# Up-projection of a hybrid layer: adding a stored product on VectorE, and weight differences on GpSimd

## Chip, core and metric

The kernel runs on one core of a Trainium2 chip. The metric is the device time of one execution in microseconds, lower is better. Engines are called TensorE (PE), VectorE (DVE), ScalarE (ACT), GpSimd (POOL) and SyncE (SP, which issues most of the DMAs). The profile's L-numbers are line numbers of the kernel before.

## What is computed

One transformer layer on a sequence of 1024 positions and a width of 1024, all in float32. It normalises the input, mixes tokens (an mLSTM head group beside sliding-window attention), adds the result to the input, and then runs a gated MLP with a short convolution. The change touches the up-projection of that MLP:

```python
def conv_ffn(h, w_up, conv_w, conv_b, w_down):
    u = causal_dwconv(h @ w_up, conv_w, conv_b)
    g, val = u[..., :D_FF], u[..., D_FF:]
    return (jax.nn.gelu(g, approximate=True) * val) @ w_down
```

D_FF is 2816, so w_up has 5632 columns: 2816 for the gate g and 2816 for val. The convolution has width 3 along positions.

## The kernel before

**Chunks.** The up-projection runs over 22 chunks (`up`, L1083). Chunk j makes 128 gate columns and the matching 128 val columns for all 1024 positions. A tile has the 128 columns as partitions and the positions along its free axis, in halves of 512.

**Seven products instead of eight.** For a chunk the 2x2 block product (two halves of the positions, gate and val, two halves of the inner dimension) is written in Strassen's way, in Winograd's form. Seven products of halves are made, each from a left side (sums and differences of the normalised input, S1 to S4, A11, A12, A22, made once) and a right side (weights, or differences of weights). Sums of products then give the four output quarters. Products are named by number 1 to 7; the dict `left` (L1038) names the left side of each. Products 4, 5, 6 and 7 use weight differences.

**Three matmuls for each k.** A float32 operand is split into a high part (a cast on ScalarE) and a remainder (a subtraction on VectorE, both in `split`, L86). One product is then 4 inner blocks by 3 matmuls (L1049 to L1051): high by high, high by remainder, remainder by high.

**Weight differences.** `up_tees` (L925) makes the four differences T of a chunk from its raw gate and val tiles (`fu` in the profile, loaded on L922): t0 = b12 - b11, t1 = b22 - t0, t2 = b22 - b12, t3 = b21 - t1, each 128x512, in L931 to L934. t1 depends on t0 and t3 on t1. There is one buffer for them (tags mix3 and mix4), so a chunk's differences wait until those of the chunk before are split. `fensure` (L938) prepares weights up to six products ahead: the T, then cast and remainder into one of a few slots (`w`, `wl`).

**Early products.** The first four chunks (`EARLY = 4`) have products 1 and 2 made ahead of the others, while the last blocks of the normalised input are still being formed (`up_early`, L1073). Product 1 is copied to the second half of the gate tile `ug` (L1078), the sum of products 1 and 2 to the first half (L1080). When `up` comes to such a chunk, an identity matmul (L1089) puts product 1 back into PSUM, and product 6 accumulates on it. The other chunks make product 1 in that same PSUM bank instead.

**Sums of products.** In `up`, `px_` and `py_` are two PSUM banks. Product 1 + 6 is copied to SBUF as u2 (L1099); product 7 is accumulated on the same bank after that. Product 5 is copied as p5 (L1101); product 3 is accumulated on its bank after that. VectorE adds p5 to `px_` (L1103) and u2 to `py_` (L1105), which gives val's tile `uv`. Product 4 then accumulates on `px_`, and the sum is copied to the second half of `ug` (L1107). All three copies are on ScalarE. The bank can't take its next product before the copy is done.

**Behind them.** The convolution (`conv3`, L1054) is one ScalarE pass and two VectorE passes per tile (L1059), twice a chunk; then GELU on ScalarE and the product with val on VectorE (L1113). After every second chunk VectorE forms sums of the activations (L1121 to L1124), which go to DRAM for the down-projection.

**Order.** Each engine runs its own queue in order. In this part of the kernel the order in each queue is written by a planner, which plays the program through in time with costs of its own before the kernel is built; the order of the source is only a preference. On TensorE the planner interleaves products of neighbouring chunks where their operands are ready.

Of the kernel before, what the change touches and what calls it, by code (L numbers as in the profile page):

```python
# [13 lines left out]
ALU = mybir.AluOpType  # L14
# [43 lines left out]
def layer_kernel(  # L58
# [18 lines left out]
    V, A, G, T = nc.vector, nc.scalar, nc.gpsimd, nc.tensor  # L77
# [22 lines left out]
    ident = cp.tile([P, P], F32, name="ident")  # L100
# [27 lines left out]
    def block_tile(b, name):  # L128
        return mixp.tile([P, MIXC], F32, tag=f"mix{b}", name=name)
# [299 lines left out]
    for k in range(KD):  # L429
# [3 lines left out]
        for i in range(0, len(todo), 4):  # L433
            for term in range(3):
                for n, b in todo[i : i + 4]:
                    h_ = hT[b // 4][term == 2][:, k, (b % 4) * P : (b % 4 + 1) * P]
                    w_ = units[2 * (k // 4) + n][term == 1][:, (k % 4) * 256 : (k % 4 + 1) * 256]
                    ps = (pkv, pv)[n][b // 2][:, 256 * (b % 2) : 256 * (b % 2 + 1)]
# [393 lines left out]
    op = tc.alloc_tile_pool(name="wout", bufs=1, side="right")  # L832
# [64 lines left out]
    EARLY = 4  # L897
# [21 lines left out]
    def up_raw(j, v, when=0):  # L919
        if (j, v, when) not in raws:  # L920
            raws[j, v, when] = w_raw(f"fu{j}_{v}_{when}")[:, :D]
            nc.sync.dma_start(raws[j, v, when], w_up[2 * j + v])  # L922
        return raws[j, v, when]

    def up_tees(j):  # L925
        if j not in tees:
            g, v = up_raw(j, 0), up_raw(j, 1)
            t12, t34 = (mixp.tile([P, MIXC], F32, tag=f"mix{3 + i}", name=f"T{j}_{i}") for i in range(2))
            t = [t12[:, :512], t12[:, 512:D], t34[:, :512], t34[:, 512:D]]
            b11, b21, b12, b22 = g[:, :512], g[:, 512:], v[:, :512], v[:, 512:]  # L930
            V.tensor_tensor(t[0], b12, b11, op=ALU.subtract)  # L931
            V.tensor_tensor(t[1], b22, t[0], op=ALU.subtract)
            V.tensor_tensor(t[2], b22, b12, op=ALU.subtract)
            V.tensor_tensor(t[3], b21, t[1], op=ALU.subtract)  # L934
            tees[j] = t
        return tees[j]

    def fensure(n):  # L938
        for at in range(len(wq), min(n, len(flat))):
            j, i = flat[at]  # L940
            src = {
                1: lambda: up_raw(j, 0, j < EARLY)[:, :512],
                2: lambda: up_raw(j, 0, j < EARLY)[:, 512:],
                3: lambda: up_raw(j, 1)[:, 512:],
                4: lambda: up_tees(j)[3],
                5: lambda: up_tees(j)[0],
                6: lambda: up_tees(j)[1],
                7: lambda: up_tees(j)[2],
            }[i]()
            w = w_slot(at, f"w{j}_{i}")  # L950
            splits.append(split(w[:, 0], w[:, 1], src))
            wq[j, i] = w

    def half_tiles(tag, name):
        t = mixp.tile([P, MIXC], F32, tag=tag, name=name)
        return t[:, :512], t[:, 512:D]
# [19 lines left out]
    for b in range(NB):  # L976
# [12 lines left out]
        t = block_tile(m, f"t{b}")[:, :D]  # L989
        A.activation(t, y, AF.Square, accum_out=ssb[:, 0, b : b + 1])  # L990
        rstd(rsb[:, 0, b : b + 1], ssb[:, 0, b : b + 1])
        t = block_tile(m, f"ty{b}")[:, :D]
# [3 lines left out]
        t = block_tile(m, f"tq{b}")[:, :D]  # L996
        A.activation(t, xb, AF.Square, accum_out=ssb[:, 1, b : b + 1])
        rstd(rsb[:, 1, b : b + 1], ssb[:, 1, b : b + 1])
        t = block_tile(m, f"tn{b}")[:, :D]
        V.tensor_scalar(t, xb, rsb[:, 1, b : b + 1], None, op0=ALU.mult)  # L1000
        ts = slice((b % 4) * P, (b % 4 + 1) * P)
        for h in range(2):
            ps = mm(f"ht{b}_{h}")
# [39 lines left out]
    def up_product(ps, j, i, first, last):  # L1043
        fensure(flat.index((j, i)) + 6)
        w, a = wq[j, i], left[i]
        for k in range(4):
            ks = slice(k * P, (k + 1) * P)
            st, en = first and k == 0, last and k == 3
            T.matmul(ps, w[:, 0, ks], a[:, 0, k, :], start=st, stop=False, skip_group_check=True)  # L1049
            T.matmul(ps, w[:, 0, ks], a[:, 1, k, :], start=False, stop=False, skip_group_check=True)  # L1050
            ends = T.matmul(ps, w[:, 1, ks], a[:, 0, k, :], start=False, stop=en, skip_group_check=True)  # L1051
        hist.append(ends)

    def conv3(src, ch, t):  # L1054
        w = lambda i: cv[:, C_FCW + 3 * ch + i : C_FCW + 3 * ch + i + 1]
        A.activation(t, src, AF.Identity, bias=cv[:, C_FCB + ch : C_FCB + ch + 1], scale=w(2))  # L1056
        for tap in (1, 0):
            sh = 2 - tap
            V.scalar_tensor_tensor(t[:, sh:], src[:, : S - sh], w(tap), t[:, sh:], op0=ALU.mult, op1=ALU.add)  # L1059
# [6 lines left out]
    def ff_tile(tag, name):  # L1066
        pool, kw = (wp, dict(bufs=1)) if tag == "ub" else (wp, dict(bufs=3)) if tag == "lo" else (mixp, {})
        n = {"ub": 4 + S, "lo": 4 * VG}.get(tag, MIXC)
        return pool.tile([P, n], F32, tag=tag, name=name, **kw)[:, :D]
# [13 lines left out]
    def up(j):  # L1083
        px_, py_ = mm(f"X{j}"), pD(f"Y{j}")
        uv = ff_tile("mix1", f"uv{j}")
        p1, p5 = half_tiles("mix2", f"q{j}")
        if j < EARLY:
            ug = gate_c[j]
            T.matmul(px_, ident, ug[:, 512:], start=True, stop=True, skip_group_check=True)  # L1089
        else:  # L1090
            ug = ff_tile("mix0", f"ug{j}")
            pz = pB(f"Z{j}")
            up_product(px_, j, 1, True, True)
            A.copy(p1, px_)
            up_product(pz, j, 2, True, True)
            V.tensor_tensor(ug[:, :512], p1, pz, op=ALU.add)
        up_product(px_, j, 6, False, True)
        u2 = p1
        A.copy(u2, px_)  # L1099
        up_product(py_, j, 5, True, True)  # L1100
        A.copy(p5, py_)  # L1101
        up_product(px_, j, 7, False, True)
        V.tensor_tensor(uv[:, 512:], p5, px_, op=ALU.add)  # L1103
        up_product(py_, j, 3, False, True)
        V.tensor_tensor(uv[:, :512], u2, py_, op=ALU.add)  # L1105
        up_product(px_, j, 4, False, True)
        A.copy(ug[:, 512:], px_)  # L1107
        yv = ff_tile("mix5", f"yv{j}")
        yg = ff_tile("mix7" if j % 2 else ("mix6", "ub")[j // 2 % 2], f"yg{j}")
        conv3(uv, NFF + j, yv)  # L1110
        conv3(ug, j, yg)
        A.activation(yg, yg, AF.Gelu_apprx_tanh)
        V.tensor_tensor(yg, yg, yv, op=ALU.mult)  # L1113
        aT[j] = yg
        if j % 2:
            r = j // 2
            e, o = aT[j - 1], aT[j]
            a11, a21, a12, a22 = e[:, :512], e[:, 512:], o[:, :512], o[:, 512:]
            tags = ("lo", "ub") if j == 1 else ("lo", "lo") if j < NFF - 1 else ("mix3", "mix4")
            s12, s4 = ff_tile(tags[0], f"s12_{r}"), ff_tile(tags[1], f"s4_{r}")[:, :512]  # L1120
            V.tensor_tensor(s12[:, :512], a21, a22, op=ALU.add)  # L1121
            V.tensor_tensor(a21, a11, a21, op=ALU.subtract)
            V.tensor_tensor(s12[:, 512:], s12[:, :512], a11, op=ALU.subtract)
            V.tensor_tensor(s4, a12, s12[:, 512:], op=ALU.subtract)  # L1124
            for p, t in ((0, e), (2, o), (4, s12)):
                nc.sync.dma_start(a_dram[p : p + 2, r].rearrange("a p c -> p a c"), t.rearrange("p (a c) -> p a c", a=2))
            nc.sync.dma_start(a_dram[6, r], s4)
# [10 lines left out]
    for j in range(NFF):  # L1138
        up(j)
# [261 lines left out]
```

## Time and profile before

| what | value |
| --- | --- |
| median of 3 runs | 1122.01 us (1121.28 to 1122.9) |
| the profiled execution | 1121.05 us, its span 1119.2 us |
| granted TensorE clock, mean | 0.998 |
| up-projection of chunks 0 to 3 on TensorE | about 492 to 548 us |
| identity matmuls (L1089) | 8 instructions for 4 products, 487.5 to 532.6 us |
| differences of weights (L931 to L934) | 88 on VectorE, 22 on each line |

The span is the time between the first and the last instruction of the profiled execution; a little time lies around it. A row of the timeline has the start in us, the duration in us, engine, line, operation, the tiles written and read, and the number of merged instructions; brackets give the idle time before it and what ended it. A row of the grouped view has the number of instructions, their busy time and mean length in ns, and the idle time before them. In a list of a line's instructions the three numbers are the least, median and greatest duration in ns.

### The profile page before, as it was taken

What the parts mean: (1) busy time and instruction counts of PE and PEld (TensorE: products, weight loads), DVE (VectorE), ACT (ScalarE), POOL (GpSimd) and SP (SyncE); (2) the same over time, 40 slices, a digit from 0 to 9 for tenths busy, and PEclk for the clock granted to TensorE, in tenths of its full rate; (3) what the DMA queues carried; (4) which work ended last, traced back from release to release, by engine and by line L of the source; (5) the groups of instructions that cost most, each with busy time, mean ns of one, the idle gap of its engine ahead of it and who ended that gap; (6) DMA issues with size and microseconds to landing.
All of it is one profiled execution on the core that took longest, in us unless ns stands there. A gap on an engine that the chain in (4) does not pass through costs nothing.

```text
span 1119.2 us, 16222 instructions
## 1 busy us (share of the span) xinstructions
PE 1108.7 (99%) x5973; PEld 942.3 (84%) x5973; DVE 844.9 (75%) x1509; ACT 563.4 (50%) x1134; POOL 147.0 (13%) x227
## 2 busy tenths in 40 slices
PE   9999999999999999999999999999999999999997
PEld 8999998888899888877788888888888888888886
DVE  6946979856664466798897879878787877776686
ACT  7732635655435355576544545454454554454552
POOL 2012335534344000000000000000000000000021
PEclk9999999999999999999999999999999999999999
DMA  9635425241104222333333133223213459633445
GB/s 362 250 125 189 131 95 189 76 150 57 38 20 150 78 76 95 114 96 111 104 123 123 57 122 123 87 81 134 104 57 112 139 189 366 223 110 104 151 130 208
DMA packets 55166, 146.85 MB, mean 131 GB/s; under 512 B 5464, under 2 KB 5808, under 8 KB 55088
## 3 DMA queue, kind: packets, MB, share of 16 engines
q1 hardware_dynamic: 53056, 140.31, 37.4%
q10 hardware_dynamic: 2032, 5.51, 1.2%
q8 instruction: 47, 0.77, 0.3%
q14 instruction: 31, 0.25, 0.1%
HBM read 117.19 MB, written 28.61 MB: 130 GB/s over the span
## 4 chain that ended last, share of the span: by engine, by line
PE 93%; DVE 2%; DMA 2%; ACT 1%; issue 1%; POOL 0%; SPq 0%; DVEq 0%; POOLq 0%; ACTq 0%
PE X L1050 7%; PE X L1049 7%; PE X L1051 7%; PE Y L1050 4%; PE Y L1051 4%; PE Y L1049 4%; PE dx L1231 3%; PE dx L1229 3%; PE dx L1230 3%; PE tg L89 3%; PE tg L90 3%; PE tg L91 3%; PE dz L1231 3%; PE dz L1229 3%; PE dz L1230 3%; PE y L89 3%
## 5 line engine op out<-in xcount | busy, mean ns | idle before, releaser
L94 POOL TENSOR_SCALAR rsb<-ssb 128x1 f32<-128x1 f32 x4 | 2.3, 577 | 606.6 <-ACT junk L1284 606.4
L1049 PE MATMUL X<-S,wl 128*128 128x512 f32 x156 | 62.5, 400 | 0.0
L1051 PE MATMUL X<-S,wl 128*128 128x512 f32 x156 | 61.7, 396 | 0.0
L1050 PE MATMUL X<-S,wl 128*128 128x512 f32 x156 | 61.6, 395 | 0.0
L1059 DVE SCALAR_TENSOR_TENSOR yg<-ug,cv,yg 128x1023 f32<-128x1023 f32 (+1 forms) x44 | 56.3, 1280 | 5.3 <-ACT yg L1056 5.3
L168 DVE SCALAR_TENSOR_TENSOR ada<-ada,cb 128x1024 f32<-128x1024 f32 x46 | 57.1, 1247 | 2.4 <-DMA ada<-in_w_ada_dram 2.3
L86 ACT CAST wl<-T 128x512 fp32r<-128x512 f32 x41 | 25.5, 623 | 66.1 <-PE X L1050 62.2
L1059 DVE SCALAR_TENSOR_TENSOR yv<-uv,cv,yv 128x1023 f32<-128x1023 f32 (+1 forms) x44 | 56.3, 1279 | 1.2 <-ACT yv L1056 1.2
L86 ACT CAST A<-ra 128x512 fp32r<-128x512 f32 x46 | 28.6, 621 | 50.4 <-PE dx L1231 20.1
L86 ACT CAST w<-T 128x512 fp32r<-128x512 f32 x47 | 29.1, 623 | 40.6 <-PE Z L1051 34.7
L1103 DVE TENSOR_TENSOR uv<-q,X 128x512 f32<-128x512 f32 x22 | 15.1, 687 | 40.3 <-PE X L1051 40.3
L86 DVE TENSOR_TENSOR w<-T,w 128x512 fp32r<-128x512 f32 x47 | 32.2, 688 | 16.4 <-ACT w L86 16.3
L86 DVE TENSOR_TENSOR A<-ra,A 128x512 fp32r<-128x512 f32 x46 | 31.6, 688 | 14.9 <-ACT A L86 14.9
L1231 PE MATMUL dx<-B,A 128*128 128x512 f32 x108 | 42.4, 393 | 0.0
L1230 PE MATMUL dx<-B,A 128*128 128x512 f32 x108 | 42.3, 391 | 0.0
L1229 PE MATMUL dx<-B,A 128*128 128x512 f32 x108 | 39.8, 394 | 0.0
L86 ACT CAST wl<-fu 128x512 fp32r<-128x512 f32 x21 | 13.1, 622 | 47.5 <-PE Y L1050 44.4
L1051 PE MATMUL Y<-S,wl 128*128 128x512 f32 x92 | 36.4, 395 | 0.0
L1049 PE MATMUL Y<-S,wl 128*128 128x512 f32 x92 | 36.4, 395 | 0.0
L1050 PE MATMUL Y<-S,wl 128*128 128x512 f32 x92 | 36.4, 395 | 0.0
L1050 PEld LDWEIGHTS X<-S,wl 128*128 128x128 f32 x156 | 29.3, 188 | 7.4 <-issue 0.5
L1049 PEld LDWEIGHTS X<-S,wl 128*128 128x128 f32 x156 | 29.3, 188 | 7.4 <-issue 0.5
(589 smaller groups left out, 3834.0 us busy)
## 6 DMA issues: line engine op xcount, KB each, us to landing
ada<-in_w_ada_dram SPq DMA_DIRECT2D x48, 512.0 KB, 4.7
ra<-a_dram SPq DMA_DIRECT2D x30, 512.0 KB, 3.9
fu<-in_w_up_dram SPq DMA_DIRECT2D x26, 512.0 KB, 3.5
a_dram<-yg SPq DMA_DIRECT2D x22, 512.0 KB, 3.7
rb<-in_w_down_dram SPq DMA_DIRECT2D x44, 256.0 KB, 4.8
fu_False<-in_w_up_dram SPq DMA_DIRECT2D x18, 512.0 KB, 3.5
a_dram<-s SPq DMA_DIRECT2D x11, 512.0 KB, 5.4
x<-in_x_dram SPq DMA_DIRECT2D x8, 512.0 KB, 6.3
```

The lines of the kernel that those rows point to most:

```text
L86: return A.copy(hi, src), eng.tensor_tensor(lo, src, f(hi), op=ALU.subtract)
L89: T.matmul(ps, lh, rh, start=first, stop=False)
L90: T.matmul(ps, lh, rl, start=False, stop=False)
L91: return T.matmul(ps, ll, rh, start=False, stop=last)
L168: return V.scalar_tensor_tensor(w, w, 0.5, cb, op0=ALU.mult, op1=ALU.mult, accum_out=mod[:, j : j + 1])
L1049: T.matmul(ps, w[:, 0, ks], a[:, 0, k, :], start=st, stop=False, skip_group_check=True)
L1050: T.matmul(ps, w[:, 0, ks], a[:, 1, k, :], start=False, stop=False, skip_group_check=True)
L1051: ends = T.matmul(ps, w[:, 1, ks], a[:, 0, k, :], start=False, stop=en, skip_group_check=True)
L1059: V.scalar_tensor_tensor(t[:, sh:], src[:, : S - sh], w(tap), t[:, sh:], op0=ALU.mult, op1=ALU.add)
L1229: T.matmul(ps[tb], a[:, 0, ts], w[:, 0], start=first and r == 0, stop=False, skip_group_check=True)
L1230: T.matmul(ps[tb], a[:, 0, ts], w[:, 1], start=False, stop=False, skip_group_check=True)
L1231: ends = T.matmul(ps[tb], a[:, 1, ts], w[:, 0], start=False, stop=last and r == NP - 1, skip_group_check=True)
```

## The change

Two things change.

First, in `up_tees` the four subtractions of chunk j go to GpSimd if j <= EARLY, else to VectorE as before. With EARLY = 4 these are chunks 0 to 4, 20 subtractions.

Second, in `up` the identity matmul of the first four chunks goes. Product 6 of these chunks starts its own accumulation in `px_`, and product 1 stays in SBUF (`c1`, the second half of `ug`). Each of the three copies out of PSUM becomes, for these four chunks, an addition of c1 on VectorE (`join`): u2, p5 and the gate's second half, which is written in place. For the other 18 chunks `join` is the ScalarE copy as before.

```diff
-            V.tensor_tensor(t[0], b12, b11, op=ALU.subtract)
-            V.tensor_tensor(t[1], b22, t[0], op=ALU.subtract)
-            V.tensor_tensor(t[2], b22, b12, op=ALU.subtract)
-            V.tensor_tensor(t[3], b21, t[1], op=ALU.subtract)
+
+            E_ = G if j <= EARLY else V
+            E_.tensor_tensor(t[0], b12, b11, op=ALU.subtract)
+            E_.tensor_tensor(t[1], b22, t[0], op=ALU.subtract)
+            E_.tensor_tensor(t[2], b22, b12, op=ALU.subtract)
+            E_.tensor_tensor(t[3], b21, t[1], op=ALU.subtract)
...
         if j < EARLY:
             ug = gate_c[j]
-            T.matmul(px_, ident, ug[:, 512:], start=True, stop=True, skip_group_check=True)
+
+            c1 = ug[:, 512:]
+            join = lambda dst, ps: V.tensor_tensor(dst, c1, ps, op=ALU.add)
         else:
             ug = ff_tile("mix0", f"ug{j}")
+            join = A.copy
...
-        up_product(px_, j, 6, False, True)
+        up_product(px_, j, 6, j < EARLY, True)
         u2 = p1
-        A.copy(u2, px_)
+        join(u2, px_)
         up_product(py_, j, 5, True, True)
-        A.copy(p5, py_)
+        join(p5, py_)
...
-        A.copy(ug[:, 512:], px_)
+        join(ug[:, 512:], px_)
```

## Prediction

> **What bounds the kernel now.** I read the page first: its header, the busy line, and the chain that ended last.
>
> ```profile
> span 1119.2 us, 16222 instructions
> ...
> PE 1108.7 (99%) x5973; PEld 942.3 (84%) x5973; DVE 844.9 (75%) x1509; ACT 563.4 (50%) x1134; POOL 147.0 (13%) x227
> ...
> PE 93%; DVE 2%; DMA 2%; ACT 1%; issue 1%; POOL 0%; SPq 0%; DVEq 0%; POOLq 0%; ACTq 0%
> ```
>
> TensorE is busy nearly all the time and is 93% of the chain. So a matmul removed can pay in full, and a TensorE that is made to wait loses in full. The share is an average, so the second view is the busy time of each engine in the stretch that the change touches, and in the one behind it.
>
> ```profile
> 484.00:537.00 53.00, 53.00 (x223) 41.54 (x222) 49.29 (x72) 31.62 (x49) 0.00 (x0) 1.00 0.24 80
> 537.00:600.00 63.00, 63.00 (x272) 50.92 (x271) 53.05 (x70) 32.16 (x47) 0.00 (x0) 1.00 0.35 117
> ```
>
> Columns: length, then TensorE, its weight loads, VectorE, ScalarE, GpSimd (instructions in brackets), granted clock 1.00. From 484 to 537 us TensorE never stops, but VectorE stops for only 53 - 49.29 = 3.7 us. GpSimd is empty. VectorE is the second bound here, and by a hair.
>
> **The identity products (removed).** Four products of 128x512 go. The timeline of TensorE, with its weight loads, shows two of them alone and two together.
>
> ```profile
> 514.36 0.39 PE L1051 MATMUL Y<-S,wl 128*128 128x512 f32 x1
> 514.59 1.02 PE L1089 MATMUL X<-ug,ident 128*128 128x512 f32 x2
> 515.05 0.79 PE L1049 MATMUL X<-S,wl 128*128 128x512 f32 x1
> 515.68 0.39 PE L1050 MATMUL X<-S,wl 128*128 128x512 f32 x1
> ...
> 487.75 1.88 PE L1089 MATMUL X<-ug,ident 128*128 128x512 f32 x4
> 489.08 0.78 PE L1049 MATMUL e<-A,w 128*128 128x512 f32 x1
> 489.70 0.40 PE L1050 MATMUL e<-A,w 128*128 128x512 f32 x1
> ...
> 489.08 0.19 PEld L1049 LDWEIGHTS e<-A,w 128*128 128x128 f32 x1 [0.28 <-ACT ug L1078]
> ```
>
> Matmuls start 514.59 - 514.36 = 0.23 us apart. From 514.59 to 515.68 are 1.09 us, of which one ordinary matmul is 0.23: one identity product costs 0.86 us. Four are 3.4 us, the upper end. The pair at 487.75 stands in a hole, though: the product behind it waits until 489.08 for a ScalarE copy (L1078) that the change leaves where it is. Without the pair the next start but one is 489.08 + 0.23 = 489.31 and not 489.70, so that pair is worth 0.4 us unless the planner finds a filler. I take 0.4 + 2 x 0.86 = **2.1 us** on TensorE, between 2.1 and 3.4.
>
> **ScalarE copies (removed).** Twelve copies out of PSUM (three for each of four chunks) leave ScalarE. It is busy 31.62 of 53 us in the stretch and no bound, so I cost the relief at nothing.
>
> **VectorE: differences out, joins in.** Timeline of VectorE, first and last of the 20 differences of chunks 0 to 4, and the group of adds out of PSUM that is the same operation as a join.
>
> ```profile
> 486.42 0.69 DVE L931 TENSOR_TENSOR T<-fu,fu 128x512 f32<-128x512 f32 x1
> 487.03 0.69 DVE L933 TENSOR_TENSOR T<-fu 128x512 f32<-128x512 f32 x1
> ...
> 535.67 0.68 DVE L934 TENSOR_TENSOR T<-fu_False,T 128x512 f32<-128x512 f32 x1
> ...
> L1103 DVE TENSOR_TENSOR uv<-q,X 128x512 f32<-128x512 f32 x22 | 15.1, 687 | 40.3 <-PE X L1051 40.3
> ```
>
> Instructions overlap a little: starts are 0.61 us apart, so I count 0.6 each. Out: 20 x 0.6 = 12.0 us, all before 537 us. In: 12 joins, x 0.6 = 7.2 us; by the places of the copies that they replace, 9 of them (5.4 us) fall before 537 us. So far VectorE gains 6.6 us in the stretch.
>
> **GpSimd: 20 subtractions of 128x512.** The stretch has none, so the nearest rows are its 128x512 products of two SBUF tiles in the mLSTM stage, with what VectorE did beside them. First the 319 us collision (GpSimd, VectorE, and that line's usual size), then the 308 us one.
>
> ```profile
> 319.05 1.27 POOL L765 TENSOR_TENSOR qw<-U,yq 128x512 f32<-128x512 f32 x1
> ...
> 319.13 1.22 DVE L800 TENSOR_TENSOR mtmp<-mtmp,gcol 128x4 f32<-128x4 f32 x1
> ...
> L800 DVE TENSOR_TENSOR mtmp<-mtmp,gcol x8: 146/160/1215, 250.6 to 341.4; 128x4 f32<-128x4 f32 x8
> ...
> 308.34 1.56 POOL L765 TENSOR_TENSOR qw<-U,yq 128x512 f32<-128x512 f32 x1 [5.16 <-PE tot L782]
> ...
> 307.53 1.23 DVE L86 TENSOR_TENSOR w20lo<-w20raw,w20hi 128x1024 fp32r<-128x1024 f32 x1 [2.10 <-ACT w20hi L86]
> 308.73 0.69 DVE L775 TENSOR_TENSOR kw<-mK,gcol 128x512 f32<-128x512 f32 x1
> 309.34 1.64 DVE L741 SCALAR_TENSOR_TENSOR yk<-ubk,cv,yk 128x1024 f32<-128x1024 f32 x1
> ...
> L741 DVE SCALAR_TENSOR_TENSOR yk<-ubk,cv,yk x12: 1277/1286/1644, 219.0 to 312.6; 128x1024 f32<-128x1024 f32 x12
> ```
>
> The four-column VectorE operation at 319.13 usually takes 0.16 us; it took 1.22 and ended at 320.35, just as the 1.27 us GpSimd product ended (320.32). At 308.34 GpSimd came while a VectorE operation ran; it took 1.56, not 1.27, so it waited 0.3 us. Then VectorE's kw, which reads one operand from PSUM, ran untouched (0.69), and the next operation on two SBUF operands took 1.64 instead of 1.29: it sat until GpSimd was done near 309.9. So an operation on two SBUF operands and a GpSimd product don't overlap; whoever starts first holds the other for the rest of its time. The Trainium skill (SBUF — State Buffer, "Who interferes with whom") states this as an exclusive port pair, and that a VectorE instruction with two SBUF inputs contends with a GpSimd instruction that reads SBUF. These rows agree; that two full queues then take turns is that rule's consequence, and no row of before shows two full queues.
>
> Here VectorE's queue is full of such operations (weight and sum remainders L86, convolution taps L1059, products, sums); only joins, the adds out of PSUM and one L1011 are not: 9 joins, 6 adds and 1, about 16 of the 61 VectorE instructions left in the stretch (72 - 20 + 9). A GpSimd subtraction gets in when a VectorE operation ends. In 45 of 61 cases the next one loses 1.27 us; otherwise 0.6 us run freely and 0.67 are lost. Mean 0.74 x 1.27 + 0.26 x 0.67 = 1.1 us, times 20 = **22 us**. Bounds: nothing (all 20 fall beside waits or PSUM reads) and 20 x 1.27 = 25.4 us.
>
> **The sum on VectorE**, 484 to 537 us: + 22 - 12.0 + 5.4 = 15.4 us more against 3.7 us of idle time, so it ends **11.7 us late** if TensorE doesn't wait for it. What waits: VectorE's queue runs in the order that the planner wrote, and behind each held operation stand the weight remainders and the joins. The joins are the tight ones. Before, the copy at their place left this much time (ScalarE copy, then the first TensorE matmul that needs the bank):
>
> ```profile
> 496.23 0.58 ACT L1099 COPY q<-X 128x512 f32<-128x512 f32 x1
> 497.84 0.39 PE L1049 MATMUL X<-S,w 128*128 128x512 f32 x1
> ...
> 525.95 0.58 ACT L1101 COPY q<-Y 128x512 f32<-128x512 f32 x1
> 529.38 0.40 PE L1049 MATMUL Y<-S,wl 128*128 128x512 f32 x1
> ...
> 536.33 0.58 ACT L1099 COPY q<-X 128x512 f32<-128x512 f32 x1
> 541.42 0.40 PE L1049 MATMUL X<-S,wl 128*128 128x512 f32 x1
> ```
>
> Slack 1.0, 2.9 and 4.5 us. At 526 us VectorE has taken 16 subtractions (17.6 us), lost 9.6 us of differences and gained 6 joins (3.6 us), and some 3.4 of its idle time is used: 8.2 us late, 2.9 covered, TensorE stalls **5.3 us**. At 537: 11.7 - 4.5 = 7.2 us. These are one delay seen twice, not two. Where VectorE sets the pace, the 2.1 us of identity products aren't earned: TensorE only waits longer. I take the lower reading, rounded to **+5 us**, since the planner, seeing VectorE lighter, may put joins earlier. Behind 537 us VectorE has 10 us of idle time in 63 and catches up, but TensorE's lost time stays lost.
>
> **Queues.** Nothing stands behind the subtractions on GpSimd (empty through the stretch). The loads of weights wait for the last difference:
>
> ```profile
> SPq L922 <- DVE T L934: 22.0, 4, 12.2
> ...
> 502.05 0.68 DVE L934 TENSOR_TENSOR T<-fu,T 128x512 f32<-128x512 f32 x1
> 505.88 0.69 DVE L931 TENSOR_TENSOR T<-fu,fu 128x512 f32<-128x512 f32 x1 [0.85 <-DMA fu<-in_w_up_dram]
> ```
>
> Chunk 1's last difference at 502.05 frees a raw buffer, and chunk 2's first waits for that load (505.88). On GpSimd four subtractions, each with up to 0.6 us of waiting, take 4 x 1.9 = 7.5 us; from about 494 us, when their tiles are free, that ends near 501.5, no later than before. Chunk 2's first product starts at 515.05, so 2 us either way are covered. Cost nothing.
>
> **Time.** Profiled execution before: 1121.05 us (span 1119.2 and 1.85 around it); the median of the runs shown is 1122.01, 0.96 higher. 1121.05 + 5 = 1126.05, on the median **1127.0 us**. About 0.2% (2.2 us) is what a measurement can tell from no change.
>
> **Rivals.** *Cover holds, faster.* If a subtraction costs VectorE under about 0.74 us (20 x 0.74 = 14.8, - 12.0 + 5.4 - 3.7 = 4.5 us late, just the last slack), TensorE mostly keeps its pace and earns 2.1 to 3.4 us: 1118.6 to 1119.9. For it: a planner that sees VectorE lighter, ScalarE half idle. Against it: the 319 and 308 us rows, and 92% busy VectorE. Chance 0.27, 0.17 of it beyond 0.2%.
> *Only the first chunk pays, same.* Chunk 0's differences are two dependent pairs.
>
> ```profile
> 491.84 1.90 DVE L86 TENSOR_TENSOR w<-T,w 128x512 fp32r<-128x512 f32 x3
> 493.17 0.40 PE L1051 MATMUL X<-S,w 128*128 128x512 f32 x1
> ```
>
> The first of three remainders ends near 492.5 and is used at 493.17, 0.7 us of slack. If GpSimd's chain of two or three (1.27 each, plus waits) makes it 1 to 4 us late, and later chunks have cover, the result is -1 to +2 us: 1121 to 1124. Chance 0.14.
> *Every subtraction costs its full 1.27 us, slower still.* 25.4 + 5.4 - 12.0 - 3.7 = 15.1 us late, less 2.9: +12, 1134. Chance 0.06.
> *The change isn't what its words say.* They speak of nine chunks; the condition j <= EARLY with EARLY = 4 takes five. I priced five.
>
> **Chances.** Forecast (VectorE becomes the bound, +2.3 to +9): 0.53. Faster by over 0.2%: 0.17; within: 0.10 + 0.14 = 0.24; slower: 0.53 + 0.06 = 0.59. The range 1118.8 to 1131.5 leaves out the edge of the faster rival and the dearest cases, about 0.2.
>
> **What would show it.** Right: VectorE operations on two SBUF operands of 1.5 to 2 us beside GpSimd's, GpSimd's 1.3 to 1.9 us long; VectorE without idle time from 484 to 540; TensorE waiting for joins. Right about the identity products: none on the page, and 0.86 us less on TensorE at each of the last two. Wrong: TensorE still without a gap, or VectorE's operations at 0.69 us beside GpSimd's.

## The result, and the profile after

| kernel | median | range | runs |
| --- | --- | --- | --- |
| before | 1122.45 us | 1121.28 to 1125.87 | 4 |
| changed | 1132.73 us | 1130.32 to 1135.05 | 4 |

The changed kernel takes 1.0086 times as long [1.0071, 1.0102], which is 9.7 us more (the two medians of the table differ by 10.3). The forecast had the sign and half the size (+5), and its range ended at 1131.5.

The profiled execution of the changed kernel took 1131.51 us. Its line numbers are two higher around the matmuls (L1051 to L1053 for one product, copies of the early products on L1080 and L1082, `up_tees` on L933 to L936, joins on L1093, the adds that make `uv` on L1108 and L1110, the product with val on L1118). First its page: header, busy line and chain of waits.

```profile
span 1129.8 us, 16214 instructions
...
PE 1112.0 (98%) x5965; PEld 943.7 (84%) x5965; DVE 851.8 (75%) x1501; ACT 556.6 (49%) x1122; POOL 184.6 (16%) x247
...
PE 87%; DVE 6%; DMA 2%; issue 2%; ACT 1%; POOL 1%; SPq 0%; POOLq 0%; DVEq 0%; ACTq 0%
```

VectorE's share of the chain grew from 2% to 6%, TensorE's fell from 93% to 87%. Next the busy time in the two stretches of the forecast (length, TensorE, weight loads, VectorE, ScalarE, GpSimd, clock, DMA), in the changed kernel:

```profile
484.00:537.00 53.00, 45.78 (x187) 35.30 (x186) 45.14 (x55) 24.27 (x39) 29.92 (x16) 0.97 0.21 63
537.00:600.00 63.00, 62.49 (x268) 50.00 (x267) 59.15 (x74) 28.60 (x40) 7.42 (x4) 1.00 0.37 124
```

TensorE had no gap from 484 to 537 us and now lacks 7.2 us. But VectorE, which the forecast wanted without idle time, is *less* busy than before: 45.14 us instead of 49.29. An engine that rests more isn't late through too much work alone: it, too, waits for something. The mean clock of the first stretch fell from 1.00 to 0.97.

TensorE's waits say for what. Comparing starts of matmuls with the usual 0.23 us shows the places at which it lost more than 0.08 us between 484 and 552 us; together they make 11.1 us. Taking off the four identity products that are gone (4 x 0.86 = 3.4) leaves 7.7 us. That is all that the stretch lost. Without the identity products both kernels have 5965 matmuls, so the nth of one can be set against the nth of the other. The 3150th starts at 459.75 us before and at 461.20 now, the 3600th at 566.27 and at 575.45: the matmuls between them take 106.5 and 114.3 us, 7.7 more. The rest of the 10.6 us by which the two spans differ lies where nothing was changed: 1.45 us ahead of the 3150th, and 1.45 in the last 965 matmuls, which take 221.1 us before and 222.5 now. The first two losses, in the timeline of the changed kernel (start, duration, engine, line, tiles, and in brackets the wait), with what the other engines did:

```profile
488.98 0.40 PE L1053 MATMUL e<-A,w 128*128 128x512 f32 x1
490.54 0.51 PE L1051 MATMUL e<-A,w 128*128 128x512 f32 x1 [1.16 <-ACT ug L1080]
...
493.17 0.39 PE L1053 MATMUL e<-A,w 128*128 128x512 f32 x1
496.20 0.50 PE L1051 MATMUL X<-S,w 128*128 128x512 f32 x1 [2.64 <-ACT w L86]
...
486.28 5.85 POOL L933 TENSOR_TENSOR T<-fu,fu 128x512 f32<-128x512 f32 x1 [6.48 <-DVE S L86]
492.09 1.74 POOL L935 TENSOR_TENSOR T<-fu 128x512 f32<-128x512 f32 x1
493.78 1.71 POOL L934 TENSOR_TENSOR T<-fu,T 128x512 f32<-128x512 f32 x1
...
486.68 0.68 DVE L966 TENSOR_TENSOR smix<-F 128x512 f32<-128x512 f32 x1
487.28 0.68 DVE L968 TENSOR_TENSOR smix<-F,F 128x512 f32<-128x512 f32 x1
...
489.09 0.67 DVE L969 TENSOR_TENSOR smix<-F,smix 128x512 f32<-128x512 f32 x1
...
491.04 1.65 DVE L86 TENSOR_TENSOR S<-smix,S 128x512 fp32r<-128x512 f32 x1
...
495.52 1.67 ACT L86 CAST w<-T 128x512 fp32r<-128x512 f32 x3 [3.48 <-POOL T L934]
```

The wait at 490.54 is the hole in which the identity pair used to stand: 490.54 - 488.98 - 0.23 = 1.33 us, now empty. The wait at 496.20 (2.8 us by the starts) is new. GpSimd's first subtraction for chunk 0 took 5.85 us, and meanwhile VectorE ran its own operations 0.60 us apart, none of them longer than usual. Only at 491.04 is one of VectorE's held, as GpSimd has got in. The third of GpSimd's differences ends at 495.49, ScalarE's cast starts at 495.52, and TensorE goes on at 496.20. GpSimd's lower speed alone would not have done this: three undisturbed differences of 1.29 us each would, by an estimate from 486.28, have ended at about 490.2, more than 5 us earlier. What made the chain late is that GpSimd was held.

The largest loss comes at 528 us. Same view, four engines:

```profile
527.88 0.40 PE L1053 MATMUL Y<-S,wl 128*128 128x512 f32 x1
531.20 0.47 PE L1051 MATMUL X<-A,w 128*128 128x512 f32 x1 [2.92 <-DVE uv L1108]
...
533.48 0.63 PE L1053 MATMUL X<-A,w 128*128 128x512 f32 x1
533.91 0.63 PE L1051 MATMUL X<-A,w 128*128 128x512 f32 x1
...
526.24 1.28 ACT L1117 ACT_TABLE_LOAD   x1 [3.40 <-DVE yg L1061]
527.54 1.06 ACT L1117 ACTIVATE yg<-yg 128x1024 f32<-128x1024 f32 x1
528.75 0.62 ACT L86 CAST wl<-T 128x512 fp32r<-128x512 f32 x1
...
527.43 1.28 POOL L934 TENSOR_TENSOR T<-fu,T 128x512 f32<-128x512 f32 x1
...
528.63 1.23 DVE L1118 TENSOR_TENSOR yg<-yg,yv 128x1024 f32<-128x1024 f32 x1 [1.86 <-ACT yg L1117]
529.77 0.68 DVE L86 TENSOR_TENSOR wl<-T,wl 128x512 fp32r<-128x512 f32 x1
530.37 0.68 DVE L1108 TENSOR_TENSOR uv<-q,X 128x512 f32<-128x512 f32 x1
```

TensorE waits for an add (L1108, 530.37) that frees its bank. The add is short, but stands in VectorE's queue behind L1118, which idled 1.86 us for GELU (ScalarE, with a 1.28 us table load ahead of it), and behind a remainder (529.77) whose cast (528.75) starts 0.04 us after GpSimd's second difference ends (527.43 + 1.28). Two chains end there within an instruction of each other. Behind the wait, matmuls start 0.43 us apart instead of 0.23 (533.48, 533.91), eight of them, 8 x 0.2 = 1.6 us more. The granted clock in the two microseconds from 533 is 0.50 in the row of each:

```profile
533.00:534.00 1.00, 1.00 (x4) 0.76 (x3) 1.00 (x1) 0.62 (x1) 1.00 (x2) 0.50 0.00 0
534.00:535.00 1.00, 1.00 (x4) 0.81 (x3) 1.00 (x2) 0.00 (x0) 1.00 (x1) 0.50 0.00 0
```

The 20 subtractions, grouped by line (busy time, mean ns of one, idle time ahead and its cause):

```profile
L933 POOL TENSOR_TENSOR T<-fu,fu 128x512 f32<-128x512 f32 x4 | 9.7, 2436 | 13.7 <-DMA fu<-in_w_up_dram 7.2 <-DVE S L86 6.5
L935 POOL TENSOR_TENSOR T<-fu 128x512 f32<-128x512 f32 x5 | 8.9, 1774 | 12.1 <-DVE w L86 12.1
L934 POOL TENSOR_TENSOR T<-fu,T 128x512 f32<-128x512 f32 x5 | 8.1, 1612 | 0.3
L936 POOL TENSOR_TENSOR T<-fu,T 128x512 f32<-128x512 f32 x4 | 7.9, 1973 | 0.1
...
L933 POOL TENSOR_TENSOR T<-fu,fu_False 128x512 f32<-128x512 f32 x1 | 1.3, 1292 | 3.8 <-DMA fu<-in_w_up_dram 3.8
```

Undisturbed, one takes 1.29 us; the one at 527.43 us above, while VectorE idled, took 1.28. GpSimd's busy time in the two stretches is 29.92 + 7.42 = 37.3 us; 20 x 1.29 = 25.8, so GpSimd was held for 11.5 us. VectorE was held as well: two of its rows beside two of GpSimd's, where the first usually takes 1.28 us and the second 0.69.

```profile
519.91 2.27 POOL L935 TENSOR_TENSOR T<-fu 128x512 f32<-128x512 f32 x1 [5.42 <-DVE w L86]
522.14 2.28 POOL L936 TENSOR_TENSOR T<-fu,T 128x512 f32<-128x512 f32 x1
...
521.55 1.72 DVE L1061 SCALAR_TENSOR_TENSOR yg<-ug,cv,yg 128x1023 f32<-128x1023 f32 x1
523.19 1.78 DVE L86 TENSOR_TENSOR w<-T,w 128x512 fp32r<-128x512 f32 x1
```

Added up over the 15 operations from 484 to 552 us that were longer than usual, VectorE lost 12.5 us: 0.63 us for each subtraction, and just about the 12.0 us that it was relieved of.

### The profile page after: what moved, and what is told of

It is laid out like the page before. It is cut to its first block, busy times and chain, and to the rows that moved or that the text cites. A ratio compares the mean times of both kernels' runs of the same rounds, so it can differ in the third digit from the quotient of the medians.

```text
span 1129.8 us, 16214 instructions
## 1 busy us (share of the span) xinstructions
PE 1112.0 (98%) x5965; PEld 943.7 (84%) x5965; DVE 851.8 (75%) x1501; ACT 556.6 (49%) x1122; POOL 184.6 (16%) x247
## 4 chain that ended last, share of the span: by engine, by line
PE 87%; DVE 6%; DMA 2%; issue 2%; ACT 1%; POOL 1%; SPq 0%; POOLq 0%; DVEq 0%; ACTq 0%
PE X L1051 6%; PE X L1053 6%; PE X L1052 6%; PE dx L1236 3%; PE dx L1234 3%; PE dx L1235 3%; PE Y L1052 3%; PE Y L1053 3%; PE Y L1051 3%; PE tg L89 3%; PE tg L90 3%; PE dz L1234 3%; PE dz L1236 3%; PE tg L91 3%; PE dz L1235 3%; PE y L89 3%
## 5 line engine op out<-in xcount | busy, mean ns | idle before, releaser
L1053 PE MATMUL X<-S,wl 128*128 128x512 f32 x156 | 61.7, 396 | 0.0
L1051 PE MATMUL X<-S,wl 128*128 128x512 f32 x156 | 61.7, 395 | 0.0
L1108 DVE TENSOR_TENSOR uv<-q,X 128x512 f32<-128x512 f32 x22 | 15.1, 686 | 42.2 <-PE X L1053 42.2
L86 DVE TENSOR_TENSOR w<-T,w 128x512 fp32r<-128x512 f32 x47 | 35.7, 763 | 13.6 <-ACT w L86 13.5
L1051 PE MATMUL X<-A,w 128*128 128x512 f32 x88 | 35.1, 399 | 2.9 <-DVE uv L1108 2.9
L1051 PE MATMUL Y<-S,wl 128*128 128x512 f32 x92 | 36.4, 396 | 0.2 <-ACT wl L86 0.2
L1053 PE MATMUL Y<-S,wl 128*128 128x512 f32 x92 | 36.4, 395 | 0.0
L1053 PEld LDWEIGHTS X<-S,wl 128*128 128x128 f32 x156 | 29.3, 188 | 7.1
```

The lines of the kernel that those rows point to most:

```text
L86: return A.copy(hi, src), eng.tensor_tensor(lo, src, f(hi), op=ALU.subtract)
```

## The experiments

Two theories went in. The **load theory** is the forecast's: VectorE loses more time to GpSimd's accesses than the 20 differences cost it, and its lateness is TensorE's. The **waiting theory** says that VectorE's load decides nothing: a chain of differences is longer on GpSimd than it was on VectorE, and TensorE waits where the result is used soon after (later expectations call this latency, or place). All times below are medians against the kernel before on the same chip, as a ratio with its 95% interval, and that ratio in microseconds of 1122.

**1. Joins alone.** All differences on VectorE, no identity products.

```diff
-            E_ = G if j <= EARLY else V
+            E_ = V
```

> The changed kernel with all weight differences back on VectorE; the identity products are gone and the joins stay. Load theory (collisions make VectorE the bound): no collisions are left, VectorE has 7.2 us more work against 3.7 us of idle time, so -1 to +2 us against the kernel before. Waiting theory (TensorE waits for GpSimd's late chain and not for VectorE's load): the identity products are earned but for the hole at 489 us, so -1 to -3 us. Either way most of the 10 us are gone; if the kernel stays at +6 us or more, the joins are the cause and both theories fall.

Measured: 0.9997 [0.9987, 1.0007], -0.3 us, within the load theory's numbers and short of the waiting theory's. In the timeline of TensorE the hole is there, as large as in the changed kernel:

```profile
490.79 0.40 PE L1053 MATMUL e<-A,w 128*128 128x512 f32 x1
492.36 0.50 PE L1051 MATMUL e<-A,w 128*128 128x512 f32 x1 [1.16 <-ACT ug L1080]
```

So without GpSimd the joins cost TensorE little. Taking the identity products out brought less than the 2.1 us of the forecast, which lies outside the interval (-1.5 to +0.8). Between the 3150th and the 3600th matmul the trace shows 1.2 us less than before, and one short wait for a join:

```profile
501.37 0.47 PE L1051 MATMUL X<-S,w 128*128 128x512 f32 x1 [0.37 <-DVE q L1093]
```

**2. GpSimd alone.** The kernel before, with its identity products, and the first five chunks' differences on GpSimd.

```diff
+            E_ = G if j <= EARLY else V
-            V.tensor_tensor(t[0], b12, b11, op=ALU.subtract)
+            E_.tensor_tensor(t[0], b12, b11, op=ALU.subtract)
...
```

> The kernel before with the 20 differences of chunks 0 to 4 on GpSimd; identity products and ScalarE copies stay. Load theory: VectorE gives up 12.0 us and loses about 22 us, has 3.7 us of idle time, 3 us of slack: +3 to +5 us. Waiting theory: chunk 0's differences come 4 to 5 us late as in the changed kernel, but the hole at 489 us is filled again by identity products: +5 to +8 us, with TensorE idle before chunk 0's first product for 2 to 4 us.

Measured: 1.0081 [1.0067, 1.0096], +9.1 us. By the medians the differences on GpSimd make the whole loss. Both theories set it lower, though the upper end of the waiting theory (+8) lies within the interval (+7.5 to +10.8). TensorE waits 2.56 us for chunk 0's differences, with half the clock behind it. The second large wait of the changed kernel is small here: 1.00 us at 531.21, where the changed kernel has 3.09. So that wait seems to need the joins in VectorE's queue as well, though each kernel has one trace only.

**3. All but chunk 0.** As the changed kernel, chunk 0's differences on VectorE.

```diff
-            E_ = G if j <= EARLY else V
+            E_ = G if 0 < j <= EARLY else V
```

> The changed kernel with chunk 0's four differences back on VectorE; chunks 1 to 4 stay on GpSimd. Load theory: a fifth of the collisions goes, so +8 us against the kernel before in place of +10. Waiting theory: the wait of 3 to 4 us before chunk 0's first product goes, so +5 to +7 us, and no GpSimd subtraction takes longer than about 2.3 us.

Measured: 1.0029 [1.0018, 1.0040], +3.3 us, below what either theory gave (+8, and +5 to +7). One chunk of five carries 9.7 - 3.3 = 6.4 us. What is left is one wait at 526 us for the add of L1108 (2.65 us by the starts), and eight matmuls at half clock behind it.

**4. Idle subtractions on GpSimd.** All differences on VectorE; GpSimd subtracts each of the 20 from itself into a tile that nobody reads. This work is added to the kernel.

```diff
+            E_ = V
...
+            if j <= EARLY:
...
+                for i in range(4):
+                    G.tensor_tensor(dummy[0], t[i], t[i], op=ALU.subtract)
```

> Joins as in the changed kernel, all differences on VectorE, and GpSimd subtracts each of the 20 from itself into a tile that nobody reads: the collisions stay, but no product waits for GpSimd. Load theory: VectorE keeps its 12 us and loses 20 x 1.1 us as well, so it is 20 us late or more: +15 us or more against the kernel before. Waiting theory: within 3 us of the kernel with joins alone, since VectorE's full queue keeps GpSimd out more than the other way round.

Measured: 1.0056 [1.0042, 1.0069], +6.3 us, which neither theory expected. GpSimd and VectorE, from two answers of the timeline:

```profile
486.74 10.21 POOL L942 TENSOR_TENSOR dummy<-T 128x512 f32<-128x512 f32 x1 [9.07 <-ACT S L86]
...
498.10 0.69 DVE L934 TENSOR_TENSOR T<-fu,fu 128x512 f32<-128x512 f32 x1 [2.05 <-POOL dummy L942]
```

The test wasn't clean: the next chunk's differences must wait until GpSimd has read the old ones, so an operation meant to be idle became one that is waited for. It does show again that GpSimd isn't let in while VectorE's queue is full: 10.21 us for its first subtraction.

**5. Chunk 0 alone.** Only its four differences go to GpSimd (`E_ = G if j == 0 else V`).

> The changed kernel with only chunk 0's four differences on GpSimd; chunks 1 to 21 on VectorE. Latency theory (TensorE waits because GpSimd's chain of differences ends late, VectorE losing little in total): the 3.5 us that TensorE waited at chunk 0's first products come back on top of the kernel with joins alone, so +3 to +5 us against the kernel before. Load theory (each collision costs VectorE 0.6 to 1.1 us): 4 collisions less 2.4 us of work saved, so within 1.5 us of the kernel with joins alone.

Measured: 1.0034 [1.0019, 1.0048], +3.8 us, as the latency theory had it. The timeline of GpSimd's first subtraction and of TensorE:

```profile
488.49 5.84 POOL L933 TENSOR_TENSOR T<-fu,fu 128x512 f32<-128x512 f32 x1 [6.48 <-DVE S L86]
...
495.38 0.39 PE L1053 MATMUL e<-A,w 128*128 128x512 f32 x1
498.40 0.50 PE L1051 MATMUL X<-S,w 128*128 128x512 f32 x1 [2.63 <-ACT w L86]
```

Against kernel 1, which differs in these four instructions alone, it costs 3.8 + 0.3 = 4.1 us: the wait of 2.79 us and slower matmuls behind it.

**6. The table load moved ahead.** The changed kernel with a one-column GELU, its result unused, behind the last early copy, so that the 1.28 us table load isn't in the chain at 526 us.

```diff
+    A.activation(gb[:, :1], gate_c[EARLY - 1][:, 0:1], AF.Gelu_apprx_tanh)
```

> The changed kernel with one GELU of a single column, result unused, behind the last early copy, so that ScalarE's table load of 1.28 us runs at about 499 us and not at 526. If the wait of 3.1 us at 528 us is the chain convolution, table load, GELU, product with val, add out of PSUM in VectorE's fixed order, it shrinks by about 1.3 us and the half clock behind it may go too: -1 to -3 us against the changed kernel, so +7 to +9 us against the kernel before. If VectorE's load alone sets that wait, nothing changes: +10 us.

Measured: 1.0103 [1.0089, 1.0118], +11.6 us; expected was less than the changed kernel's 9.7. The timeline of VectorE shows why nothing was won:

```profile
528.40 1.23 DVE L1118 TENSOR_TENSOR yg<-yg,yv 128x1024 f32<-128x1024 f32 x1 [0.59 <-ACT yg L1117]
531.43 0.69 DVE L86 TENSOR_TENSOR wl<-T,wl 128x512 fp32r<-128x512 f32 x1 [1.80 <-ACT wl L86]
532.04 0.68 DVE L1108 TENSOR_TENSOR uv<-q,X 128x512 f32<-128x512 f32 x1
```

The product with val now idles 0.59 us instead of 1.86, but the remainder behind it idles 1.80 us for the other chain: GpSimd's second difference, 2.28 us long here, then the cast. The add behind both is as late as before. In the changed kernel the two chains tied, so shortening one shows nothing. The 1.9 us between the two kernels are not clear of the noise: their intervals overlap.

**7. The same number of chunks, later.** Chunks 5 to 9 instead of 0 to 4.

```diff
+            E_ = G if EARLY < j <= 2 * EARLY + 1 else V
```

> The changed kernel with GpSimd making the differences of chunks 5 to 9 in place of 0 to 4: the same 20 subtractions, where VectorE has 17% idle time and weights are prepared further ahead. Latency theory: the longer chain is covered, so within 1.5 us of the kernel with joins alone, -1 to +1.5 us against the kernel before. Load theory with 0.6 us lost to each and 0.6 saved: the same. If collisions cost wherever they fall, +3 us or more.

Measured: 0.9992 [0.9981, 1.0003], -0.9 us, the best median of all, though not apart from the kernel before. One stretch of it, columns as above:

```profile
600.00:700.00 100.00, 100.00 (x433) 81.03 (x432) 85.06 (x104) 47.77 (x71) 14.12 (x8) 1.00 0.32 111
```

Eight subtractions take 14.12 / 8 = 1.77 us each, so they are held by VectorE as before, and TensorE has no gap. The number of subtractions is the same; the place is another. This doesn't part the two theories, both of which expected it: VectorE has more idle time here (15 us in these 100). It does show that collisions cost nothing where there is such room: VectorE's longer operations lost 16 us in all beside these 20 subtractions, more than the 12.0 us that it was relieved of.

**8. Identity products kept for two chunks.** Differences all on VectorE; chunks 0 and 1 as before, chunks 2 and 3 with joins, so that the hole stays filled.

```diff
+            join = A.copy if j < 2 else lambda dst, ps: V.tensor_tensor(dst, c1, ps, op=ALU.add)
+            if j < 2:
+                T.matmul(px_, ident, c1, start=True, stop=True, skip_group_check=True)
```

> Joins and no identity product for chunks 2 and 3 only; chunks 0 and 1 keep the identity product and the copies; all differences on VectorE. The identity pair of chunks 0 and 1 fills the hole of 1.3 us at 489 us that the kernel with joins alone shows, the other two cost 0.86 us each in the kernel before: -1 to -2 us against the kernel before, and no wait at 489 us. If the hole is no loss, the same as with joins alone, -0.3 us.

Measured: 1.0002 [0.9991, 1.0014], +0.2 us, a miss. TensorE has no wait from 460 to 600 us, and two identity products, 0.86 us each by the forecast's rows, are gone. Yet the time is that of before. The trace shows that the 1.7 us were won and lost again elsewhere: from the 3150th matmul to the 3600th this kernel takes 104.8 us, 1.8 less than before, and the last 965 matmuls take 222.8 us against 221.1. The edit touches nothing there, and some of the other kernels show the same; why is open.

**9. Nine chunks, as the words say** (`E_ = G if j <= 2 * EARLY else V`).

> The changed kernel with GpSimd making the differences of chunks 0 to 8, nine as its words say. Place theory (GpSimd's differences cost where weights are prepared just in time, not later): the 16 added subtractions are as free as those of chunks 5 to 9, so the same as the changed kernel, +9 to +11 us against the kernel before. Load theory: 16 more collisions against the same savings, +12 us or more if VectorE is still behind from the first chunks.

Measured: 1.0090 [1.0067, 1.0113], +10.1 us, no different from five.

**10 and 11. Half of the differences.** Chunks 1 to 4 only; in 10 the first pair (t0, t1) on GpSimd, in 11 the second (t2, t3). The diff is that of 10.

```diff
+            E_ = G if 0 < j <= EARLY else V
...
+            V.tensor_tensor(t[2], b22, b12, op=ALU.subtract)
+            V.tensor_tensor(t[3], b21, t[1], op=ALU.subtract)
```

> As the kernel without chunk 0 on GpSimd (+3.2 us), but of chunks 1 to 4 only the first two differences (t0, t1) are on GpSimd; t2 and t3 are on VectorE. If what costs there is that the next loads wait for GpSimd's last difference (t3), this returns to +0 to +1.5 us. If collisions cost, half of them stay: +1.5 to +2 us.

> The other half: of chunks 1 to 4 only t2 and t3 are on GpSimd. If the loads that wait for t3 are what costs, it stays at +2.5 to +4 us. If collisions cost, half of them stay: +1.5 to +2 us.

Measured: 1.0009 [0.9997, 1.0021], +1.0 us, and 0.9999 [0.9986, 1.0013], -0.1 us. Neither account, loads or collisions, fits kernel 11. By the medians either half is nearly free and both together cost +3.3, but the intervals are too wide to say whether that is more than a sum. The traces say more. By the starts of matmuls TensorE waits 0.16 us for the add of L1108 in kernel 1, then, in kernel 10 (first row) and kernel 11 (second row):

```profile
523.72 0.47 PE L1051 MATMUL X<-A,w 128*128 128x512 f32 x1 [1.02 <-DVE uv L1108]
526.81 0.47 PE L1051 MATMUL X<-A,w 128*128 128x512 f32 x1 [0.87 <-DVE uv L1108]
```

That is 1.17 and 1.03 us by the starts, and 2.65 in kernel 3. So the waits come near a sum; what only the long one has is the half clock behind it. Kernel 11 also speaks against the loads of the weights as the cause, which wait for t3 in 11 as in 3.

**12. Kernel 3 with the early table load of kernel 6.**

> The kernel without chunk 0 on GpSimd (+3.2 us) with the early one-column GELU. There the wait of 2.7 us at 526 us stands behind table load, GELU and product with val in VectorE's order, and GpSimd's chain of chunk 3 is not tied with it. If so, the wait shrinks by the table load's 1.3 us and the half clock behind it goes too (1.5 us): 0 to +2 us against the kernel before. If another chain is as late, as in the changed kernel, it stays at +3 us.

Measured: 1.0016 [1.0005, 1.0028], +1.8 us. TensorE's wait for that add, in the view of waits (total, times, longest), first in kernel 3:

```profile
PE X L1051 <- DVE uv L1108: 2.5, 1, 2.5
```

and in kernel 12:

```profile
PE X L1051 <- DVE uv L1108: 1.2, 1, 1.2
```

It is half as long, and no matmul behind it runs at half clock, as expected. Without chunk 0's delay the chain through GELU is the longer of the two, and shortening it does show. The intervals of 3 and 12 overlap, so by the medians the 1.5 us between them are likely rather than certain; the traces show 1.6 us.

**All kernels in one table.** The first column is the measured difference against the kernel before. The second is the difference in the time from the 3150th to the 3600th matmul, in the one profiled execution of each; it leaves out what varies elsewhere, such as the last 965 matmuls (221.1 to 222.8 us).

| kernel | median, us | 3150th to 3600th matmul, us |
| --- | --- | --- |
| changed | +9.7 | +7.7 |
| 1, joins alone | -0.3 | -1.2 |
| 2, GpSimd alone | +9.1 | +5.8 |
| 3, all but chunk 0 | +3.3 | +2.3 |
| 4, idle subtractions | +6.3 | +7.5 |
| 5, chunk 0 alone | +3.8 | +3.0 |
| 6, table load ahead | +11.6 | +8.3 |
| 7, chunks 5 to 9 | -0.9 | -1.1 |
| 8, two identity products | +0.2 | -1.8 |
| 9, nine chunks | +10.1 | +9.2 |
| 10, first pair | +1.0 | +0.9 |
| 11, second pair | -0.1 | -0.2 |
| 12, kernel 3 and table load | +1.8 | +0.7 |

In the second column kernels 1 and 2 make 4.6 us together and the changed kernel 7.7, so in these traces some 3 us come only where the joins and the late differences meet.

## Why the prediction had the sign and missed the size

The sign came out right for a reason that the forecast had not priced, so that much was luck. The path to it, VectorE late through its own load, is not what the runs show. Of its signs of being right, VectorE's operations of 1.5 to 2 us beside GpSimd's came true; VectorE without idle time and TensorE waiting for joins didn't. From 486.7 to 491.0 us VectorE ran at its usual 0.68 us beside a waiting GpSimd, which was one of its signs of being wrong.

- **The price of a subtraction on VectorE (1.1 us, 22 us in all) was wrong.** Measured: 0.63 us and 12.5 us in all. The step supposed that a subtraction gets in when a VectorE operation ends. No row of before showed two full queues, and in the changed kernel VectorE goes on undisturbed while GpSimd waits (486.28 us). The forecast's own threshold for "cover holds" was 0.74 us, so by its logic the kernel would have come out faster. It came out slower, so VectorE's load isn't what decides. Kernel 5 says the same: four subtractions cost 4.1 us against kernel 1, where the load theory gave at most 1.5.
- **"Queues: cost nothing" was the step that failed.** It gave each subtraction up to 0.6 us of waiting, and the first one waited 4.6 (5.85 - 1.29). It asked when the loads and chunk 2's first product need the results, 2 us either way, and left chunk 0's first product, with 0.7 us of slack, out of the sum. The rival "only the first chunk pays" held the mechanism: it put GpSimd 1 to 4 us late at 493.17 us, and the wait for the same product in the changed kernel (496.20) is 2.8 us. It set the sum at -1 to +2 us, since it counted the identity products as won and later chunks as covered. Measured: 4.1 us for chunk 0 alone, 6.4 us as its part of the change.
- **Later chunks: +3.3 us (kernel 3), not covered.** The forecast looked for joins to be late. In the changed kernel TensorE waits for no join; the one large wait is for an add that the planner had queued behind a product and a remainder, both held up by chains that pass through GpSimd or ScalarE (kernels 6 and 12). Joins were waited for only where other delays were gone: 0.4 us in kernel 1, 1.3 in kernel 10, 0.6 in kernel 12.
- **Half clock: no term for it.** In the changed kernel it is 1.6 us of the 7.7; kernel 5 has it behind chunk 0's wait as well.
- **Identity products: 2.1 us forecast, 0.3 us by the medians and 1.2 in the trace of kernel 1.** The hole at 487.75 us was read rightly, as it stands empty at 490.79 us in kernel 1. The other two products bring their 1.7 us where the hole stays filled (1.8 in the trace of kernel 8); in kernel 1 short waits behind the joins take part of it back, 0.53 us by the starts at 501.37.
- **Five chunks or nine:** no matter, as kernel 9 shows.
- **A reading:** the 92% busy VectorE of the rivals is 93% by its row (49.29 of 53 us), which changes nothing.

What stays open beside this: why the last 965 matmuls take up to 1.7 us more in some kernels, and a proof apart from the traces that the 5.85 us are the shared access to SBUF. The length comes back in the kernels that have chunk 0's differences on GpSimd (5.84 us in kernel 5), and the subtraction at 527.43 us, with VectorE idle, takes 1.28, but no run took VectorE's operations away at this place to see the length vanish.

## What to carry to other kernels

Ask of work that moves to a slower engine when its result is used, before asking what it relieves, and whether that engine gets in at all beside a full queue: 20 subtractions cost 9.1 us where their results were due at once, and nothing five chunks later. In a queue with a fixed order a late operand also delays everything behind it, and where two chains tie, shortening one shows nothing until the other is shorter too. And where an operation stands in a hole, taking it out leaves an empty hole.

## What the runs showed of the hardware

- **A full VectorE queue doesn't take turns with GpSimd.** For 4.6 us (486.4 to 491.0) VectorE's operations on SBUF operands followed each other 0.60 us apart, and a GpSimd subtraction of 1.29 us took 5.85; with a longer stretch of the same kind it took 10.21 (kernel 4). In the changed kernel GpSimd gets in at VectorE's first gap, just ahead of 491.04 us. Over the 20 subtractions both lose: 11.5 us on GpSimd (4.6 of them here), 12.5 on VectorE. The Trainium skill (SBUF — State Buffer, "Who interferes with whom") says that whoever issues first has the shared pair for its whole instruction. That the next instruction of the same queue comes ahead of a waiting GpSimd is read from these traces.
- **A wait of TensorE can cost a second time.** After 10 of the 12 waits of 1.96 to 3.57 us in this stretch of these kernels (by the starts of matmuls, less 0.23) the granted clock fell to 0.50, and up to eight matmuls started 0.43 us apart; after waits up to 1.5 us never. Two waits, of 2.8 us (changed kernel, 496.20) and 2.61 us (kernel 9), passed without it. The Trainium skill (TensorE: Matmul & The Clock Gate, "Part 1: The HAM clock gate (the "warmup" mystery)") gives half rate after an idle window of about 3.4 us that runs freely; the runs show it behind shorter waits too, and that it doesn't follow every wait fits a window that isn't tied to them.
